# A hybrid decoder layer on one core: queries split two units ahead, sample steps emitted when their operands are due, and a planner that counts fp32 products as two passes

## The chip, the cores and the metric

The kernel runs on one core of a Trainium2 chip. The metric is the device time of one execution in microseconds; a time is the median of several runs. The engines are TensorE (PE, with its weight loads PEld), VectorE (DVE), ScalarE (ACT), GpSimd (POOL) and SyncE (SP, which here only issues DMAs). ACT and POOL issue DMAs too, in line with their other instructions.

## What is computed

One transformer-like layer for two groups of requests with the same weights: a prompt of 1024 tokens and 8 sample requests of 8 tokens, each with a cache of 4096 tokens in 32 pages. Cut to what matters:

```
h = rms_norm(x) * (1 + scale1) + shift1          # scale, shift, gate from the conditioning c
z = h @ w_in                                     # q, keys, values, gates, conv and pool inputs
k_cmp, v_cmp = compress(cache blocks of 32)      # silu(block @ w1) @ w2, for prompt and caches
o_cmp, p_cmp = attention over compressed blocks
top_i = the 16 best cache blocks of 64 by p_cmp  # samples; a prompt of 1024 has only 16 blocks
o_slc = attention over the selected blocks
o_win = attention over a window of 512
o_attn = g0 * o_cmp + g1 * o_slc + g2 * o_win
x = x + gate1 * (concat[o_attn, conv mixer, pooling mixer] @ w_out)
x = x + gate2 * swiglu(rms_norm(x) * (1 + scale2) + shift2)
```

All of it is float32. Products that need the precision are made as three products of rounded halves (`mm3`: high by high, high by low, low by high, on "float32r" tiles, whose names end in h, hi, l or lo); others are plain float32 products.

## The kernel before

The program has five stretches: the conditioning, the first norm and the input projection, with the compression of three caches (0 to 393 us of the profile); the attention (393 to 861); the output projection with the second norm; the product up of the FFN; the product down.

**Tasks and the planner's clock.** The program is written by generators ("tasks"). `run` always continues the task of the lowest priority number that is due by the planner's own clock: `self.t` holds a time for each engine, `use` adds the planner's cost of an operation to its engine, `mm` that of a product to "pe", and a task that yields a time is continued when that time is at most `MARGIN` (1.2 us) behind "pe". `hold` yields until a condition is true, `bank_of` until a PSUM bank is free. So the costs of the planner have no effect on the chip but through the order in which instructions are written. In the attention stretch that order is kept on PE (`self.turn`), and on DVE, ACT and POOL (the class `InTurn`), in the kernel before as well. Ahead of it and behind it the Tile scheduler orders the instructions.

**Prompt attention** (`prompt_attention`, `scores`): 32 units, for each of 8 blocks of 128 queries two halves of the heads, and for each half a unit "slc" (selected and compressed keys, tile `P`) and a unit "win" (window, tile `Pw`). A unit makes scores (`kh,qh`, `kl,qh`, `kh,ql`), masks them with DVE (`P<-bank`, with the running minimum in `st`), takes exponentials with ACT (`P<-P,st`), scales them with POOL (`P<-P,st` again), transposes with PE (`ident,P`), copies to `pt` with ACT or DVE, multiplies by values (`pt,vt`) and evacuates to `mo`, which goes to the DRAM tile `mix_d`. `query_parts` splits the queries of a block in `qh` (ACT) and `ql` (DVE).

**Compression** (`compress`, `compress_post`): eight pages at a time ("octet", tile `stream`, read by a gather of which SP's queue issues six pages and POOL's two) times `w1`; then an add (DVE), a silu (ACT, which loads a table for it), products by `w2`, a square root (another table), and key and value to `cmp_d`. Five of the eight caches are compressed during the attention.

**Sample attention** (`sample_select`, `sample_attention`, `sample_values`, `sample_combine`): for each of four pairs of requests, `sample_select` scores compressed keys, finds the blocks with a chain on DVE (`scr`, `mx8`, `bias`), then 9 units of cache or window are scored (`unit,qb`, `stream,qb`), exponentiated (`e`), transposed and multiplied by the values (`spt`), and `sample_combine` adds the 12 parts with weights (`cw`) into `co`, by one DVE instruction for each part, transposes it, and sends it (`smo`) to `mix_d`.

**Output projection** (`output_projection`): loads `wout` (tile `w_raw`, split into `w_hi` and `w_lo`), loads the mixer outputs back from `mix_d` (`mixc`, split into `mh` and `ml`), and x (`x1a`, `x1b`) by `x_load`.

Of the kernel before, what the change touches and what calls it, by code (L numbers as in the profile page):

```python
# [85 lines left out]
class Kernel:  # L86
# [43 lines left out]

    def ready(self, tag):

        return min(self.free[tag]) if self.free[tag] else self.t["pe"] + 0.25
# [16 lines left out]
    def mm(self, out, lhsT, rhs, start, stop, chain=False):  # L150
        n = 1
        for s in rhs.shape[1:]:
            n *= s
        if lhsT.dtype == F32:
            cost = 4 * max(n, 128) / 2400
            if lhsT.shape[-1] <= 64:
                cost *= 0.55 if lhsT.shape[-1] > 32 else 0.27
        else:
            cost = max(n, 256 if lhsT.dtype == F32R and n > 1 else n) / 2400
            if lhsT.shape[0] <= 64:  # L160
                cost *= 0.55
        self.t["pe"] += cost
        return self.in_turn(lhsT.shape[0] <= 64,
                            lambda: self.nc.tensor.matmul(out, lhsT, rhs, start=start, stop=stop, skip_group_check=chain))  # L164
# [393 lines left out]
    def gather(self, dst, name, b, p0, n, share=0):  # L558
# [10 lines left out]
        r = self.use("pool", share * 1.04, self.t["pe"])  # L569
# [8 lines left out]
    def compress(self, pool, batches, ahead):  # L578
# [5 lines left out]
        for b in batches:  # L584
# [5 lines left out]
            for half in range(2):  # L590
                uv = (yield from self.bank_of("S")).rearrange("p (v n) -> p v n", v=2)
                for q in range(2):
# [12 lines left out]
                    if i + 2 <= last:  # L605
                        self.compress_load(i + 2)
# [50 lines left out]
    def compress_post(self, pool, b, vt, pre, r, w=256):  # L657
        nc = self.nc
        nc.vector.tensor_tensor(pre[:, :, 0:w - 1], pre[:, :, 0:w - 1], vt[:, :, 1:w], op=OP.add)
        r = self.use("dve", 0.1 + w * 0.0023, r)  # L660
        nc.scalar.activation(vt[:, :, 0:w], pre[:, :, 0:w], AF.Silu, bias=self.pec[:, 0:1])
# [39 lines left out]
        self.give(self.cmp_tags[0], r)  # L701
        nc.vector.reciprocal(sq, sq)
# [348 lines left out]
    def prompt_attention(self, pool):  # L1051
        units = [(j, half, br) for j in range(8) for half in range(2) for br in ("slc", "win")]
        self.acc = None
        yield self.stacks_at
        for u, (j, half, br) in enumerate(units):
            if half == 0 and br == "slc":
                if j:
                    self.query_parts(self.query_pool, j)
            yield from self.scores(pool, u, j, half, br)

    def query_parts(self, pool, j):

        self.query_pool = pool
        self.qs = [pool.tile([P, 4, P], F32R, name=x, bufs=2) for x in ("qh", "ql")]
        self.split(*self.qs, self.q[:, :, j * P:(j + 1) * P], 512)
# [181 lines left out]
    def sample_select(self, pool, p, st):  # L1247
# [7 lines left out]
        yield from self.hold(lambda: self.cmp_done >= 2 * p + 2 and self.selected == p)  # L1255
# [17 lines left out]
        nc.scalar.activation(pc[:, 1:256], S[:, 0:NCMP], AF.Exp, bias=m0[:, 0:1], accum_out=m0[:, 1:2])  # L1273
        sn = pool.tile([P, 2, 64], F32, name="sn", bufs=2)
        for j, x in enumerate((8, 10)):
            nc.vector.tensor_tensor_reduce(out=sn[:, j], in0=S2[:, 64 * j:64 * j + 64], in1=self.m_new[:, p],
                                           scale=-1.0, scalar=3e38, op0=OP.add, op1=OP.min, accum_out=nm[:, x:x + 1])
        for j, x in enumerate((8, 10)):
            nc.scalar.activation(sn[:, j], sn[:, j], AF.Exp, scale=-1.0, bias=nm[:, x:x + 1], accum_out=den[:, x:x + 1])
        nc.vector.reciprocal(m0[:, 1:2], m0[:, 1:2])  # L1280
# [6 lines left out]
        r = self.use("dve", 2.0, self.t["pe"])  # L1287
        self.give("S", self.use("act", 1.0, self.t["pe"], table="exp"))
        self.give("S", r)
# [3 lines left out]
        self.mm(g[:, 32:96], self.rsum, i4, True, True)  # L1293
        ga = pool.tile([P, 3, 8], F32, name="ga", bufs=2)
# [32 lines left out]
        for b2 in range(2):  # L1327
            r = self.rows(b2)
            for h in range(2):
                n = P if h == 0 else NCMP - P  # L1330
                self.mm(o[r, 0:P], ct[:n, h, r], kv[b2][:n, h, P:2 * P], h == 0, h == 1)
        nc.scalar.activation(part[:, 11], o[:, 0:P], AF.Copy)
# [33 lines left out]
    def sample_attention(self, pool):  # L1366
# [9 lines left out]
        for u in range(36):  # L1376
            p, x = divmod(u, 9)
            st = sts[p]
            if x == 0 and p < 3:
                if p > 0:  # L1380
                    yield from self.hold(lambda: self.combined >= p)
# [54 lines left out]
    def sample_combine(self, pool, st, p):  # L1436
# [9 lines left out]
        for x, (a, b) in enumerate(br):  # L1446
            nc.vector.tensor_reduce(ds_[:, x:x + 1], nm[:, a:b], axis=AX.X, op=OP.min)
        for x, (a, b) in enumerate(br):
            nc.scalar.activation(w[:, a:b], nm[:, a:b], AF.Exp, scale=-1.0, bias=ds_[:, x:x + 1])
        nc.vector.tensor_tensor(dd[:, 0:11], w[:, 0:11], den[:, 0:11], op=OP.mult)  # L1450
# [7 lines left out]
        nc.vector.tensor_scalar(o, part[:, 11], gr[:, 0:1], None, op0=OP.mult)  # L1458
        for c in (0, 1, 2, 3, 4, 5, 6, 7, 8, 10):
            nc.vector.scalar_tensor_tensor(o, part[:, c], w[:, c:c + 1], o, op0=OP.mult, op1=OP.add)  # L1460
        yield self.use("dve", 3.7, self.t["pe"])
        yield from self.hold(lambda: "last" in st)
        nc.vector.scalar_tensor_tensor(o, part[:, 9], w[:, 9:10], o, op0=OP.mult, op1=OP.add)
        yield self.use("dve", 0.3, st["last_at"]) + 0.2
        tr = yield from self.bank_of("S")
        self.tr(tr[:, 0:P], o)
        mo = pool.tile([P, 4, 2, NT], F32, name="smo", bufs=2)
# [63 lines left out]
    def output_projection(self, wp, pool, nt, x1, opened):  # L1531
# [44 lines left out]
        def x_load(n=2):  # L1576
            for c, k in xq[:n]:
                dst, src = x1["load"](c, k)
                (nc.gpsimd if c == 0 else nc.scalar).dma_start(dst, src)
# [783 lines left out]
```

## Time and profile before

| | us |
|---|---|
| median of 3 runs (1707.48 to 1709.27) | 1708.68 |
| the profiled execution, its own time | 1700.77 |
| its span | 1699.2 |
| PE busy in the span | 1570.5 (92%) |
| DVE, ACT, POOL busy | 1098.5, 771.7, 665.4 |
| mean granted clock of TensorE | 0.962 |

PE is the engine that is busiest in each stretch. A PE that is not busy waits for another engine or a DMA. The granted clock is 1 at 2.4 GHz and 0.5 at 1.2 GHz. The profiled execution took 7.9 us less than the median of the timed runs.

### The profile page before, as it was taken

What the parts mean: (1) busy time and instruction counts of PE and PEld (TensorE: products, weight loads), DVE (VectorE), ACT (ScalarE), POOL (GpSimd) and SP (SyncE); (2) the same over time, 40 slices, a digit from 0 to 9 for tenths busy, and PEclk for the clock granted to TensorE, in tenths of its full rate; (3) what the DMA queues carried; (4) which work ended last, traced back from release to release, by engine and by line L of the source; (5) the groups of instructions that cost most, each with busy time, mean ns of one, the idle gap of its engine ahead of it and who ended that gap; (6) DMA issues with size and microseconds to landing.
All of it is one profiled execution on the core that took longest, in us unless ns stands there. A gap on an engine that the chain in (4) does not pass through costs nothing.

```text
span 1699.2 us, 35607 instructions
## 1 busy us (share of the span) xinstructions
PE 1570.5 (92%) x12697; PEld 1400.4 (82%) x12697; DVE 1098.5 (65%) x2638; ACT 771.7 (45%) x1821; POOL 665.4 (39%) x801
## 2 busy tenths in 40 slices
PE   6999999998897899899779989999999999899988
PEld 2988987897675666556479979999999999899988
DVE  4723354665564576766559887776777776476695
ACT  3521135324565566665548544333444343344462
POOL 3120111104332233322111365554555555688695
PEclk9899999998898999989989989999999999999999
DMA  9575756306464255234496735446444335967553
GB/s 342 195 260 165 199 173 214 128 10 193 141 187 137 79 160 174 78 103 130 156 328 213 235 131 191 147 143 230 144 144 144 143 141 202 390 240 242 189 172 120
DMA packets 183314, 302.12 MB, mean 178 GB/s; under 512 B 24305, under 2 KB 110898, under 8 KB 182818
## 3 DMA queue, kind: packets, MB, share of 16 engines
q1 hardware_dynamic: 163586, 270.96, 48.3%
q0 software_dynamic: 6624, 18.60, 3.5%
q10 hardware_dynamic: 12928, 10.29, 1.9%
q8 instruction: 101, 1.65, 0.4%
q14 instruction: 75, 0.61, 0.1%
HBM read 233.43 MB, written 70.53 MB: 179 GB/s over the span
## 4 chain that ended last, share of the span: by engine, by line
PE 69%; DVE 12%; DMA 6%; ACT 5%; issue 4%; POOL 2%; SPq 1%; ACTq 0%; DVEq 0%; POOLq 0%
PE bank L164 66%; PE bank L169 3%; DVE w_lo L208 2%; DMA stream<-in_cacheA 1%; DVE x L1918 1%; DVE P L78 1%; SPq L568 1%; DMA w_raw<-in_wup 1%; DMA x1b<-in_xT 1%; ACT Pw L78 1%; DMA wada<-in_wada 1%; ACT P L78 1%; POOL w_s L208 1%; DVE d_lo L208 1%; DVE pt L78 1%
## 5 line engine op out<-in xcount | busy, mean ns | idle before, releaser
L164 PE MATMUL bank<-b_lo,w_hi 128*128 128x272 f32 x1232 | 355.3, 290 | 2.5 <-DVE b_lo L208 2.5
L164 PE MATMUL bank<-b_hi,w_hi 128*128 128x272 f32 x1232 | 352.1, 291 | 5.3 <-DVE f_g L1716 2.9
L164 PE MATMUL bank<-b_hi,w_lo 128*128 128x272 f32 x1232 | 350.3, 290 | 1.2 <-DVE w_lo L208 1.2
L164 PEld LDWEIGHTS bank<-b_hi,w_hi 128*128 128x128 f32 x1232 | 231.8, 190 | 8.1 <-ACT b_hi L212 3.9
L164 PEld LDWEIGHTS bank<-b_lo,w_hi 128*128 128x128 f32 x1232 | 234.1, 190 | 3.4 <-DVE b_lo L208 3.4
L164 PEld LDWEIGHTS bank<-b_hi,w_lo 128*128 128x128 f32 x1232 | 232.3, 190 | 1.4 <-DVE w_lo L208 1.4
L208 DVE TENSOR_TENSOR w_lo<-w_raw,w_hi 128x512 fp32r<-128x512 f32 (+2 forms) x121 | 116.1, 970 | 64.0 <-ACT w_hi L212 63.5
L208 POOL TENSOR_TENSOR w_s<-w_raw 128x512 f32<-128x512 f32 (+1 forms) x88 | 125.0, 1421 | 69.9 <-DVE w_lo L208 52.7
L212 ACT ACTIVATE w_hi<-w_raw 128x512 fp32r<-128x512 f32 (+2 forms) x122 | 80.6, 678 | 148.3 <-PE bank L164 99.8
L164 PEld LDWEIGHTS bank<-stream 128*128 128x128 f32 x1056 | 131.9, 205 | 18.9 <-issue 10.5
L164 PE MATMUL bank<-stream 128*128 128x128 f32 x1056 | 137.6, 291 | 10.0 <-DMA stream<-in_cacheA 6.5
L208 POOL TENSOR_TENSOR x<-x,d_m 128x272 f32<-128x272 f32 x144 | 124.6, 885 | 36.5 <-DVE x L1918 20.2
L164 PE MATMUL bank<-h_hi,w_hi 128*128 128x384 f32 (+1 forms) x384 | 129.8, 338 | 0.0
L164 PE MATMUL bank<-g,w_hi 128*128 128x272 f32 x616 | 122.1, 294 | 6.6 <-DVE x L1918 5.4
L164 PE MATMUL bank<-h_hi,w_lo 128*128 128x384 f32 (+1 forms) x384 | 127.7, 333 | 0.0
L164 PE MATMUL bank<-h_lo,w_hi 128*128 128x384 f32 (+1 forms) x384 | 126.5, 329 | 0.0
L208 DVE TENSOR_TENSOR w_lo<-w_s,w_hi 128x512 fp32r<-128x512 f32 (+1 forms) x124 | 115.3, 933 | 15.6 <-ACT w_hi L212 13.4
L164 PE MATMUL bank<-g,d_hi 128*128 128x272 f32 x616 | 119.2, 290 | 4.5 <-DVE x L1918 2.3
L1918 DVE SCALAR_TENSOR_TENSOR x<-bank,mod,x 128x272 f32<-128x272 f32 (+1 forms) x192 | 86.6, 474 | 38.8 <-PE bank L164 35.6
L164 PEld LDWEIGHTS bank<-g,w_hi 128*128 128x128 f32 x616 | 98.7, 192 | 8.4 <-DVE x L1918 6.0
L1746 POOL TENSOR_TENSOR f_g<-f_g,f_v 128x272 f32<-128x272 f32 x44 | 44.0, 999 | 152.1 <-DVE f_v L1716 131.0
L78 POOL TENSOR_SCALAR P<-P,st 128x128 f32<-128x128 f32 (+14 forms) x120 | 63.7, 547 | 101.3 <-DVE st L78 91.8
(387 smaller groups left out, 3826.4 us busy)
## 6 DMA issues: line engine op xcount, KB each, us to landing
g_d<-f_s SPq DMA_DIRECT2D x57, 544.0 KB, 3.4
g<-g_d SPq DMA_DIRECT2D x56, 544.0 KB, 6.8
wada<-in_wada SPq DMA_DIRECT2D x96, 256.0 KB, 5.4
stream<-in_cacheA SPq DMA_DIRECT2D x192, 128.0 KB, 3.2
w_raw<-in_wup SPq DMA_DIRECT2D x40, 512.0 KB, 4.3
unit<-in_cacheB SPq DMA_DIRECT2D x152, 128.0 KB, 2.3
stream<-in_cacheB SPq DMA_DIRECT2D x104, 128.0 KB, 2.3
w_raw<-in_wout SPq DMA_DIRECT2D x24, 512.0 KB, 4.6
```

The source lines that it names most:

```text
L78: r = f(*args, **kwargs)
L164: lambda: self.nc.tensor.matmul(out, lhsT, rhs, start=start, stop=stop, skip_group_check=chain))
L169: return self.in_turn(ident.shape[0] <= 64, lambda: self.nc.tensor.transpose(out, in_, ident))
L208: (self.nc.vector if eng == "dve" else self.nc.gpsimd).tensor_tensor(out, a, b, op=op)
L212: self.nc.scalar.activation(hi, src, AF.Copy)
L568: eng.dma_start(dst[:, a + j, :], self.i[name][bass.ds(regs[j], 1)].rearrange("n p f -> (n p) f"))
L1746: nc.gpsimd.tensor_tensor(g[:, 1], s1, v, op=OP.mult)
L1918: nc.vector.scalar_tensor_tensor(out[:, :n], acc[:, :n], self.mod[:, 5, m, 0:1], out[:, :n], op0=OP.mult, op1=OP.add)
```

## The change

It has four parts, and none adds or removes an operation; two copies to `pt` go to DVE instead of ACT.

- The planner's costs: a plain float32 product is counted as two passes instead of four (`mm`), a page that POOL gathers as 0.6 us instead of 1.04 (`gather`).
- `when(t)`: a new yield until t less MARGIN, put ahead of steps of the compression and of the samples, so that they are written only when the planner's clock has come to their operands. The sums of `sample_combine` are written one at a time. The steps of `sample_select` are costed one by one, and their exponentials are written behind the masks.
- The queries of block j + 1 are split at the start of the second half of block j, two units ahead, instead of at the start of block j + 1.
- The wait until the pair before is combined moves from `sample_attention` (where it held up the units too) to the `sample_select` of the pair behind. All of `x_load` goes by POOL's queue; before it were the first four of 16, and ACT's queue took the other 12.

```
         if lhsT.dtype == F32:
-            cost = 4 * max(n, 128) / 2400
+            cost = 2 * max(n, 128) / 2400
...
+    def when(self, t):
+
+        yield t - MARGIN
...
-        r = self.use("pool", share * 1.04, self.t["pe"])
+        r = self.use("pool", share * 0.6, self.t["pe"])
...
                     if i + 2 <= last:
+                        yield from self.when(self.t["pe"])
                         self.compress_load(i + 2)
...
     def compress_post(self, pool, b, vt, pre, r, w=256):
         nc = self.nc
+        yield from self.when(r)
         nc.vector.tensor_tensor(pre[:, :, 0:w - 1], pre[:, :, 0:w - 1], vt[:, :, 1:w], op=OP.add)
         r = self.use("dve", 0.1 + w * 0.0023, r)
+        yield from self.when(r)
         nc.scalar.activation(vt[:, :, 0:w], pre[:, :, 0:w], AF.Silu, bias=self.pec[:, 0:1])
...
             if half == 0 and br == "slc":
-                if j:
-                    self.query_parts(self.query_pool, j)
+                self.qs = self.next_qs
+            if half == 1 and br == "slc" and j < 7:
+                self.query_parts(self.query_pool, j + 1)
...
-        self.qs = [pool.tile([P, 4, P], F32R, name=x, bufs=2) for x in ("qh", "ql")]
-        self.split(*self.qs, self.q[:, :, j * P:(j + 1) * P], 512)
+        self.next_qs = [pool.tile([P, 4, P], F32R, name=x, bufs=2) for x in ("qh", "ql")]
+        self.split(*self.next_qs, self.q[:, :, j * P:(j + 1) * P], 512)
...
-        yield from self.hold(lambda: self.cmp_done >= 2 * p + 2 and self.selected == p)
+        yield from self.hold(lambda: self.cmp_done >= 2 * p + 2 and self.selected == p and self.combined >= p - 1)
...
             if x == 0 and p < 3:
-                if p > 0:
-                    yield from self.hold(lambda: self.combined >= p)
                 self.spawn(1, self.sample_select(pool, p + 1, sts[p + 1]))
...
+        self.use("dve", 1.2, self.t["pe"])
         for c in (0, 1, 2, 3, 4, 5, 6, 7, 8, 10):
+            yield from self.when(self.t["dve"])
             nc.vector.scalar_tensor_tensor(o, part[:, c], w[:, c:c + 1], o, op0=OP.mult, op1=OP.add)
-        yield self.use("dve", 3.7, self.t["pe"])
+            self.use("dve", 0.28)
         yield from self.hold(lambda: "last" in st)
+        yield from self.when(st["last_at"])
...
-                (nc.gpsimd if c == 0 else nc.scalar).dma_start(dst, src)
+                nc.gpsimd.dma_start(dst, src)
```

Three places where the order of instructions moves. The first is ACT at the start of the second block of queries, in the attention's first microseconds. Before, the split `qh` stands behind the evacuations of an octet (`vt`), two table loads and the exponentials of the block ahead:

```order
L78 ACT_TABLE_LOAD
L78 ACTIVATE ksq<-bank,eps 128x256
L78 ACTIVATE vt<-bank 64x128 x4
L78 ACTIVATE mo<-bank 128x256
L78 DMA mix_d<-mo 128x2x128
L78 ACT_TABLE_LOAD
L78 ACTIVATE P,st<-P,st 128x128 x2
L78 ACTIVATE P,st<-P,st 128x7 x2
L78 ACTIVATE qh<-q 128x512
L78 ACTIVATE Pw,st<-Pw,st 128x128 x4
```

Now (the split of the same block, on ACT too):

```order
L78 ACTIVATE P,st<-P,st 128x128 x2
L78 ACTIVATE P,st<-P,st 128x7 x2
L78 ACTIVATE P,st<-P,st 128x128 x2
L78 ACTIVATE P,st<-P,st 128x7 x2
L78 ACTIVATE qh<-q 128x512
L78 ACTIVATE vt<-bank 64x128 x4
L78 ACTIVATE Pw,st<-Pw,st 128x128 x4
L78 ACTIVATE P,st<-P,st 128x128 x2
L78 ACTIVATE P,st<-P,st 128x7 x2
L78 ACTIVATE pt<-bank 7x512
L78 ACT_TABLE_LOAD
```

`qh` has gone ahead of the table loads and of the exponentials of the second half of its predecessor.

The second place is DVE in the first `sample_combine`, in the middle of the attention (`cw` the weights, `co` the sum, `Pw,st<-bank` the mask of a prompt unit's scores, `ISA st` the read of its minimum). Before:

```order
L78 TENSOR_TENSOR cs<-cs,gr 128x2
L78 TENSOR_SCALAR cw<-cw,cs 128x9
L78 TENSOR_SCALAR cw<-cw,cs 128x2
L78 TENSOR_SCALAR co<-part,gr 128x128
L78 SCALAR_TENSOR_TENSOR co<-part,cw,co 128x128 x10
L78 ISA Pw,st<-bank,m_edge 128x320
```

Now (on DVE, the last part of the same combine):

```order
L78 SCALAR_TENSOR_TENSOR co<-part,cw,co 128x128
L78 ISA e,nm<-bank,bias 128x512
L78 ISA nm 128x1
L78 RECIPROCAL ksq<-ksq 128x256
L78 SCALAR_TENSOR_TENSOR kvo<-ko,c_kgain,ksq 128x2x128
L78 SCALAR_TENSOR_TENSOR co<-part,cw,co 128x128
L78 COPY pt<-bank 128x8x64 x2
L78 RECIPROCAL st<-st 128x2
L78 TENSOR_TENSOR st<-st,gates 128x2
L78 RECIPROCAL st<-st 128x2
L78 TENSOR_TENSOR st<-st,gates 128x2
L78 SCALAR_TENSOR_TENSOR co<-part,cw,co 128x128 x8
```

The ten sums stood in one run; now sample masks, a key's normalisation, copies to `pt` and steps of `st` stand between the first of them, and the last eight are a run still.

The third place is POOL at the end of the attention (`P` and `Pw` are the scalings of the last two prompt units, `smo` the samples' result, `x1a` and `x1b` the loads of x, `mixc` the loads of the mixer outputs that the first projection products need). Before:

```order
L78 TENSOR_SCALAR P<-P,st 128x1024 x2
L78 DMA mix_d<-smo 128x4x16
L78 TENSOR_SCALAR P<-P,st 128x1024 x2
L78 TENSOR_SCALAR Pw<-Pw,st 128x640 x2
L78 TENSOR_SCALAR Pw<-Pw,st 128x63 x2
L78 TENSOR_SCALAR Pw<-Pw,st 128x640 x2
L78 TENSOR_SCALAR Pw<-Pw,st 128x63 x2
L78 DMA mix_d<-smo 128x4x16
L1553 DMA mixc<-mix_d 128x2x272 x4
L1579 DMA x1a_10598<-in_xT 128x2x272 x4
```

Now (POOL, the same place):

```order
L78 TENSOR_SCALAR P<-P,st 128x1024 x2
L78 DMA mix_d<-smo 128x4x16
L78 TENSOR_SCALAR P<-P,st 128x1024 x2
L1600 DMA x1a_10598<-in_xT 128x2x272 x4
L1600 DMA x1a_10599<-in_xT 128x2x272 x4
L1600 DMA x1b<-in_xT 128x2x272 x6
L78 TENSOR_SCALAR Pw<-Pw,st 128x640 x2
L78 TENSOR_SCALAR Pw<-Pw,st 128x63 x2
L78 TENSOR_SCALAR Pw<-Pw,st 128x640 x2
L78 TENSOR_SCALAR Pw<-Pw,st 128x63 x2
L1574 DMA mixc<-mix_d 128x2x272 x4
L1600 DMA x1b<-in_xT 128x2x272 x2
```

Fourteen loads of x stand ahead of the last four scalings, the samples' result has left ahead of the last `P`, and no `smo` stands behind the scalings any more.

## Rows read from the trace of the kernel before

**Rows 1.** Busy time of each engine in six stretches of the span (columns: stretch and its length; for each engine busy us and instructions; granted clock; busy share of the DMA engines; GB/s).

```profile
0.00:100.00 100.00, 83.38 (x536) 63.28 (x537) 52.01 (x101) 41.69 (x81) 24.58 (x38) 0.95 0.77 266
100.00:393.00 293.00, 278.44 (x1889) 253.73 (x1887) 134.57 (x206) 86.14 (x158) 39.46 (x68) 0.98 0.52 158
393.00:841.00 448.00, 395.99 (x3954) 279.29 (x3954) 280.68 (x1192) 266.38 (x740) 134.74 (x244) 0.93 0.46 138
841.00:1020.00 179.00, 151.44 (x1119) 148.50 (x1120) 148.19 (x309) 97.31 (x224) 59.50 (x63) 0.90 0.69 228
1020.00:1450.00 430.00, 428.12 (x3403) 426.12 (x3402) 312.75 (x486) 168.83 (x340) 219.57 (x195) 1.00 0.47 166
1450.00:1699.20 249.20, 233.11 (x1803) 229.44 (x1802) 170.26 (x345) 111.31 (x281) 187.56 (x196) 0.98 0.65 222
```

**Rows 2.** What PE waited for between 393 and 841 us (waiting engine, what it was to write, its line, what it waited for: us in total, times, longest us).

```profile
PE bank L164 <- ACT qh L78: 21.0, 7, 5.3
PE bank L164 <- DVE pt L78: 6.3, 5, 2.7
PE bank L169 <- ACT pt L78: 3.5, 2, 2.8
PE bank L164 <- ACT vt L78: 3.2, 1, 3.2
...
PE bank L164 <- DVE ql L78: 1.8, 2, 1.5
```

**Rows 3.** The timeline of all engines around the first of the seven waits for `qh`, and PE's next wait of over 1 us (columns: start us, length us, engine, line, operation; in brackets the engine's idle time ahead of it and what ended it).

```profile
419.20 3.84 PE L164 MATMUL bank<-stream 128*128 128x128 f32 x32
...
426.06 1.28 ACT L78 ACT_TABLE_LOAD   x1 [0.48 <-ACT mo L78]
...
427.36 0.40 ACT L78 ACTIVATE P<-P,st 128x128 f32<-128x128 f32 x1
...
428.71 0.61 ACT L78 ACTIVATE qh<-q 128x512 fp32r<-128x512 f32 x1
...
429.36 0.69 DVE L78 TENSOR_TENSOR ql<-q,qh 128x512 fp32r<-128x512 f32 x1 [3.01 <-ACT qh L78]
429.38 0.63 PE L164 MATMUL bank<-kh,qh 64*128 64x320 f32 x2 [5.27 <-ACT qh L78]
...
447.16 0.65 PE L164 MATMUL bank<-pt,vt__286 128*64 128x256 f32 x4 [2.67 <-DVE pt L78]
```

**Rows 4.** The five stretches at half clock that follow a wait for `qh`, and the sum over all eleven stretches at half clock behind a wait in the attention (columns as in rows 1; the sum names its engines).

```profile
428.00:434.80 6.80, 5.42 (x26) 4.21 (x27) 4.15 (x24) 5.34 (x28) 0.00 (x0) 0.50 0.26 82
...
537.20:544.00 6.80, 5.24 (x26) 2.98 (x28) 4.46 (x18) 0.10 (x2) 1.73 (x3) 0.50 0.10 39
588.40:595.20 6.80, 5.40 (x38) 3.76 (x39) 2.96 (x15) 3.98 (x11) 0.00 (x0) 0.50 0.07 5
...
690.80:694.20 3.40, 3.40 (x25) 2.51 (x22) 2.83 (x15) 0.53 (x2) 0.85 (x2) 0.51 0.00 0
...
752.30:755.70 3.40, 3.30 (x12) 1.70 (x14) 2.51 (x8) 0.61 (x2) 0.54 (x2) 0.50 0.48 190
sum 61.20, PE 53.34 PEld 36.08 DVE 40.02 ACT 33.04 POOL 12.20; mean PE 4.85 PEld 3.28 DVE 3.64 ACT 3.00 POOL 1.11
```

**Rows 5.** The timeline around the first `sample_combine` (columns as in rows 3).

```profile
607.05 0.81 ACT L78 ACTIVATE P<-P,st 128x640 f32<-128x640 f32 x1
...
608.63 3.45 DVE L78 SCALAR_TENSOR_TENSOR co<-part,cw,co 128x128 f32<-128x128 f32 x9
...
609.30 1.05 ACT L78 ACTIVATE pt<-bank 128x512 f32<-128x512 f32 x2
...
609.92 1.59 PE L169 MATMUL bank<-ident,Pw 64*128 64x64 f32 x16 [2.81 <-ACT pt L78]
```

**Rows 6.** The timeline of POOL at the end of the attention (columns as in rows 3).

```profile
808.03 2.21 POOL L78 TENSOR_SCALAR P<-P,st 128x1024 f32<-128x1024 f32 x2 [0.34 <-DVE st L78]
811.42 2.19 POOL L78 TENSOR_SCALAR Pw<-Pw,st 128x640 f32<-128x640 f32 x4 [1.18 <-DVE st L78]
...
853.06 0.80 POOL L78 DMA_DIRECT2D mix_d<-smo  x1 [36.48 <-DVE smo L78]
853.85 2.84 POOL L1553 DMA_DIRECT2D mixc<-mix_d  x4
856.69 2.11 POOL L1579 DMA_DIRECT2D x1a<-in_xT  x3
```

**Rows 7.** The timeline of the other engines at the end of the attention (columns as in rows 3; ACTq is ACT's queue of DMAs).

```profile
801.25 0.68 DVE L78 CUSTOM_DVE_ANT_0 P<-bank,m_slc 128x512 f32<-128x512 f32 x1
...
850.12 1.15 ACT L212 ACTIVATE w_hi<-w_raw 128x512 fp32r<-128x512 f32 x2 [2.35 <-DMA w_raw<-in_wout]
...
851.39 0.34 DVE L78 SCALAR_TENSOR_TENSOR co<-part,cw,co 128x128 f32<-128x128 f32 x1
...
851.79 0.48 PE L169 MATMUL bank<-ident,co 128*128 128x128 f32 x1 [11.37 <-DVE co L78]
...
852.88 2.44 ACTq L1579 DMA_DIRECT2D x1a<-in_xT  x4
...
860.61 1.50 PE L164 MATMUL bank<-mh,w_hi 128*128 128x272 f32 x5 [8.34 <-ACT mh L212]
```

**Rows 8.** PE's products with `stream` between 100 and 393 us, the compression in the projection's stretch (columns: operation, shapes, count; busy us, mean ns; idle before and its releasers).

```profile
L164 PE MATMUL bank<-stream 128*128 128x128 f32 x448 | 56.8, 284 | 8.6 <-DMA stream<-in_cacheA 5.2 <-ACT stream L198 2.9 <-DVE cy L848 0.6
```

More of the change, by code (lines that the diff above doesn't have):

```diff
@@ L701, in compress_post @@
         self.give(self.cmp_tags[0], r)
+        yield from self.when(r)
         nc.vector.reciprocal(sq, sq)
@@ L1272, in sample_select @@
         nc.vector.memset(pc[:, 256:257], 0.0)
-        nc.scalar.activation(pc[:, 1:256], S[:, 0:NCMP], AF.Exp, bias=m0[:, 0:1], accum_out=m0[:, 1:2])
+        t = self.use("dve", 0.35, self.t["pe"] + 0.1)
         sn = pool.tile([P, 2, 64], F32, name="sn", bufs=2)
@@ L1277, in sample_select @@
                                            scale=-1.0, scalar=3e38, op0=OP.add, op1=OP.min, accum_out=nm[:, x:x + 1])
+        t2 = self.use("dve", 0.3)
+        yield from self.when(t)
+        nc.scalar.activation(pc[:, 1:256], S[:, 0:NCMP], AF.Exp, bias=m0[:, 0:1], accum_out=m0[:, 1:2])
+        self.use("act", 0.5, t + 0.1, table="exp")
         for j, x in enumerate((8, 10)):
             nc.scalar.activation(sn[:, j], sn[:, j], AF.Exp, scale=-1.0, bias=nm[:, x:x + 1], accum_out=den[:, x:x + 1])
+        t = self.use("act", 0.66, t2 + 0.1)
+        yield from self.when(t)
         nc.vector.reciprocal(m0[:, 1:2], m0[:, 1:2])
@@ L1286, in sample_select @@
         nc.vector.tensor_reduce(i4, im.rearrange("p (j c) -> p j c", c=4), axis=AX.X, op=OP.add)
-        r = self.use("dve", 2.0, self.t["pe"])
-        self.give("S", self.use("act", 1.0, self.t["pe"], table="exp"))
-        self.give("S", r)
+        r = self.use("dve", 1.3, t + 0.1)
+        self.give("S", t)
+        self.give("S", t)
         yield r + 0.8
@@ L1293, in sample_select @@
         self.mm(g[:, 32:96], self.rsum, i4, True, True)
+        yield from self.when(self.t["pe"])
         ga = pool.tile([P, 3, 8], F32, name="ga", bufs=2)
@@ L1331, in sample_select @@
                 self.mm(o[r, 0:P], ct[:n, h, r], kv[b2][:n, h, P:2 * P], h == 0, h == 1)
+        yield from self.when(self.t["pe"])
         nc.scalar.activation(part[:, 11], o[:, 0:P], AF.Copy)
@@ L1447, in sample_combine @@
             nc.vector.tensor_reduce(ds_[:, x:x + 1], nm[:, a:b], axis=AX.X, op=OP.min)
+        yield from self.when(self.use("dve", 0.3))
         for x, (a, b) in enumerate(br):
             nc.scalar.activation(w[:, a:b], nm[:, a:b], AF.Exp, scale=-1.0, bias=ds_[:, x:x + 1])
+        yield from self.when(self.use("act", 0.5, table="exp") + 0.1)
         nc.vector.tensor_tensor(dd[:, 0:11], w[:, 0:11], den[:, 0:11], op=OP.mult)
@@ L1466, in sample_combine @@
         self.tr(tr[:, 0:P], o)
+        yield from self.when(self.t["pe"])
         mo = pool.tile([P, 4, 2, NT], F32, name="smo", bufs=2)
```

## The prediction

> **What bounds the kernel now.** I read the stretches first [rows 1]: PE is busy 1570.5 us of 1699.2, and where it isn't is uneven. In the FFN's product up it idles 1.9 us of 430 and runs at full clock: nothing can be won there by order. In the attention it idles 448.0 - 396.0 = 52.0 us, at a granted clock of 0.93, while DVE, ACT and POOL are busy for 281, 266 and 135 of the 448 us. None of these is full, so PE's idle time there is a matter of who stands behind whom. Between 841 and 1020 it idles 27.6, at 0.90. Then I read what PE waited for in the attention [rows 2]: one row is 40% of it, the seven waits for `qh`, 21.0 us, and 1.8 more for `ql`. The rest, 52.0 - 22.8 - 0.6 (the 0.6 us of the end that lies before 841) = 28.6 us, has many causes; `pt` and `vt` are 6.3 + 3.5 + 3.2 = 13.0 of it.
>
> The timeline shows why `qh` is late [rows 3]. The split needs only queries that exist since the projection. But it is written at the start of its block, and ACT runs what was written ahead of it first: a table load of 1.28 us, four exponentials for `P`, then `qh` at 428.71. PE starts 0.06 us behind its end, after 5.27 us of nothing.
>
> A wait costs twice: behind five of the seven waits the granted clock is 0.5 for 3.4 to 6.8 us [rows 4]. PE was busy 5.42 + 5.24 + 5.40 + 3.40 + 3.30 = 22.8 us in these. If that work took half at the full clock, the loss is 11.4 us. All eleven such stretches hold 53.3 us of PE's work, so the other six hold 30.5 and lose 15.3.
>
> The sample steps show the second pattern [rows 5]. `sample_combine` puts one run of ten sums on DVE, 3.45 us for nine; PE's transposes need `pt`, whose copies ACT can start only at 609.30, behind the exponentials for `P` of a later unit, while DVE is shut. PE waits 2.81 us.
>
> The third place is the end [rows 7]: PE waits 11.37 us for `co`, because the sums stand between splits of `w_out`, which wait for landings (2.35 us in the row of `w_hi`), and then 8.34 us for `mixc`, which POOL's queue can fetch only once `smo` has left [rows 6]. That is 19.7 us.
>
> **The change, part by part.** *Queries, two units ahead.* The same 0.61 us on ACT and 0.69 on DVE, eight times, earlier. The second pair of buffers is free then, as the last block's scores are done by the second half. So the seven waits go: at most 22.8 + 11.4 = 34.2 us. At least nothing: ACT still has the table loads and exponentials ahead of what PE needs next. How much of the gain stays depends on the next wait, and those are rare: 52 us of idle time in 448. Behind the first wait PE ran for 15 us before another of over 1 us, from 429.4 to 447.16 - 2.67 = 444.5 [rows 3]. What it does there (more scores, sample scores, an octet of 3.84 us of products, rows 3) asks nothing of ACT's late queue, and during these ACT catches up. I take 70% of 34.2: **-24**.
>
> *`when` and the halved cost of fp32 products.* The planner's clock was about right: 16 products of an octet are 32 instructions and take 3.84 us [rows 3], 0.24 each, where the formula said 0.21. Now it says 0.11. So where the new clock leaves room of 1 us between a step and what needs it, PE holds up to 2 us of real work, as long as there is other work to put there. No instruction gets faster. The pool of gain is the other waits, 28.6, and their clock, 15.3: 43.9 together. Bounds: -44, and 0 or above if the room for samples is taken from the prompt's steps. In the new order the copies to `pt`, the largest of these waits, have no more room than before, and the last eight sums of `co` are one run still. I take 30%: **-13**.
>
> *The end.* The samples finish ahead of the last prompt units, so the 11.37 us for `co` can't come last any more. In their place stand fourteen loads of x on POOL ahead of the last four scalings of `Pw`. In the trace a load takes POOL 2.11 / 3 = 0.70 us [rows 6], so 9.8 in all; `Pw`'s scalings, which began at 811.42, 1.2 us behind the last of `P`, would be 8.6 later, and behind them stand transposes, `pt`, values, `mix_d`, then `mixc` (8.34 as before). Also PE had other work from there to 840.4 (851.79 - 11.37), the samples' among it, that hid those steps. The samples' part is now done earlier, so the same steps stand barer. Bounds: -11.4 (the loads leave while POOL would have waited for ACT's exponentials) to +8.6 (the loads are felt whole, and the bare steps take what `co` took). I take **-1.5**, the sum of -11.4, of the 8.6 and of 1.3 for the bare steps, the least certain term.
>
> The Trainium skill, PSUM — Partial Sum Buffer (section "Engine vs sequencer instructions"), says that the queues of ScalarE, VectorE and GpSimdE are strict FIFO. The trace agrees: `mixc` left POOL only behind a `smo` that had waited for 36.48 us. By this rule alone, without the -11.4, the end would be 8.6 us slower and the whole sum 10.1 us smaller, which the range holds.
>
> *Twelve loads of x from ACT's queue to POOL's.* 2.44 / 4 = 0.61 us each on ACT, 0.70 on POOL [rows 6, 7]: 8.4 us more on POOL, which between 841 and 1020 is busy 59.5 of 179 us [rows 1], so they are hidden beyond the fourteen costed above. If that cover were gone, it would be 12 x 0.09 = 1.1 us. The skill's DMA: Bandwidth & Descriptors ("Issuing engine by pattern") gives simple loads to Sync, and 1 us against 0.6 to a first byte; an estimate by that page is 0.4 us once. No row here shows it.
>
> *The front and the FFN.* The front holds 8.6 us of waits at `stream` [rows 8], mostly for gathers, and the order of the octets changes there. Bounds: -8 (nearly all of them) to +6 (two octets side by side wait 3 us each). I take **-2**. The FFN's order stays within a few swaps of neighbours; 0, with 2 us to both sides, from idle times of 1.9 and 16.1 [rows 1].
>
> **Sum.** -24 - 13 - 1.5 - 2 = -40.5. The profiled execution took 1700.8; so the changed one 1660.3. The median lies 7.9 above its profile, and 1708.7 - 40.5 = **1668**. Own range: queries from -15 to -34, samples from -3 to -25, the end -11 to +9, as independent terms, some 18 around it: 1650 to 1686.
>
> **Rivals.**
> *The gains are given back.* ACT stays as late as it was; PE runs its scores 5 us earlier and then waits at `ident,P` for exponentials that still come at the old time. For it: `qh` stood behind just these exponentials. Against it: few waits follow. With a third of the queries' gain (-11), 10% of the others (-4) and the end at +3 it is -12: 1697.
>
> *Slower: the samples' work is spent too early.* Their products are what PE does while a prompt unit's softmax is under way; from the first mask of a unit (801.25) to its scaled `P` (808.03 + 2.21 = 810.24) there are 9.0 us [rows 6, 7]. Counting fp32 as half makes the planner put more of this work behind each wait, so it runs out sooner. Each unit left without it bares up to 9.0 us. It decides from 40.5 / 9.0 = 4.5 units on; with six it is +13.5: 1722. Against it: in the new order the sample products reach to the last two units of 32. For it: those two are bare now, at the place where POOL's queue is longest.
>
> *Nothing changes.* The chip's waits follow ACT's and DVE's real lateness, which no cost of the planner knows, and shift by a few us: 1708. Against it: the seven waits have one cause, which is gone.
>
> **How the numbers follow.** Gain as summed, or more, 0.68; given back, 0.13; nothing, 0.06; slower, 0.13. What a measurement of this kernel can tell from no change is about 0.2%, 3.4 us. Faster 0.68 + 0.13 = 0.81; same 0.06; slower 0.13. The range reaches from 1645, below which I leave 0.08 (most of the 78 us of waits and clock in the attention gone), to 1706, above which lie no more than the two last cases with 0.12 of their 0.19, some of "nothing" ending within it.
>
> **What would show it.** Right: no wait of PE for `qh` or `ql` in the attention (22.8 before); a granted clock there of 0.95 or more (0.93); the attention's PE idle at 25 to 35 us (52); no `ident,co` wait at the end, and `mh,w_hi` still waited for, by 15 to 25 us in the last steps together, with fourteen loads ahead of `Pw` on POOL. The FFN alike within 2 us. Wrong: new waits of PE for `P` exponentials or `pt` that sum up to as much as `qh` did; a bare stretch of PE over 30 us at the attention's end; octets in the front that wait for gathers by more than 8.6 us.

## The result, and the profile after

The changed kernel takes 1699.5 us (median of 10 runs, 1695.7 to 1706.8); the kernel before took 1709.0 beside it (10 runs, 1704.7 to 1713.6). The ratio is 0.9946, with a 95% interval of 0.9929 to 0.9963: 9.5 us faster, where 40.5 were forecast. The direction is right, but three quarters of the gain are missing, and the time lies inside the outer range alone (1645 to 1706), not inside the prediction's own (1650 to 1686).

The stretches of the changed kernel from 100 us on (columns as in [rows 1]):

```profile
100.00:393.00 293.00, 272.46 (x1822) 246.82 (x1822) 130.99 (x191) 84.73 (x152) 36.77 (x58) 0.97 0.50 152
393.00:841.00 448.00, 395.24 (x3948) 281.03 (x3946) 290.62 (x1225) 262.89 (x730) 148.47 (x265) 0.93 0.51 151
841.00:1020.00 179.00, 163.05 (x1212) 156.30 (x1213) 147.50 (x298) 101.79 (x231) 61.64 (x63) 0.91 0.64 207
1020.00:1450.00 430.00, 426.86 (x3390) 424.46 (x3389) 311.81 (x483) 168.85 (x340) 220.46 (x197) 1.00 0.47 165
1450.00:1697.20 247.20, 231.37 (x1791) 228.19 (x1789) 171.62 (x345) 111.05 (x279) 187.52 (x194) 0.98 0.65 221
```

Between 393 and 841 PE idles 52.8 us at 0.93, against 52.0 at 0.93 [rows 1]. Nothing seems to have changed there. What it waits for has (columns as in [rows 2], 393 to 860 us):

```profile
PE bank L168 <- DVE pt L78: 9.7, 7, 3.0
PE bank L173 <- POOL Pw L78: 6.8, 1, 6.8
PE bank L173 <- ACT e L78: 5.6, 2, 5.3
PE bank L168 <- ACT w_hi L216: 5.6, 1, 5.6
PE bank L173 <- DVE st L78: 5.4, 6, 2.0
PE bank L173 <- POOL P L78: 4.2, 5, 1.7
PE bank L168 <- ACT pt L78: 4.0, 4, 2.0
```

No row for `qh` or `ql` is left of 22.8 us. In their place stand waits for `e`, `st`, `P` and `pt` that were not there or were shorter (rows of before for `P`, `e` and `st` stand under before_again). The front tells another part: the first score starts at 398.2 us, not at 391.2 as before, with as many octets compressed ahead of it. Two of PE's waits in it (timeline, columns as in [rows 3]):

```profile
287.81 1.65 PE L168 MATMUL bank<-h_sq,mean_h 128*128 128x384 f32 x2 [4.20 <-ACT h_sq L804]
...
319.29 1.06 PE L168 MATMUL bank<-wada,sc 128*32 128x256 f32 x2 [6.35 <-DMA wada<-in_wada]
```

And the end, from the timeline of the changed kernel (POOL, ACT and PE):

```profile
826.34 5.79 POOL L1600 DMA_DIRECT2D x1a<-in_xT  x8
...
837.40 4.35 POOL L78 TENSOR_SCALAR Pw<-Pw,st 128x640 f32<-128x640 f32 x8
841.19 1.97 PE L173 MATMUL bank<-ident,Pw 64*128 64x64 f32 x32 [6.83 <-POOL Pw L78]
...
856.22 0.43 ACT L216 ACTIVATE mh<-mixc 128x272 fp32r<-128x272 f32 x1 [2.43 <-DMA mixc<-mix_d]
...
858.25 3.21 ACT L216 ACTIVATE w_hi<-w_raw 128x512 fp32r<-128x512 f32 x6
...
858.92 0.59 PE L168 MATMUL bank<-mh,w_hi 128*128 128x272 f32 x1 [5.57 <-ACT w_hi L216]
```

This is the end as forecast. The fourteen loads of x hold POOL from 826.3 to 837.4, PE waits 6.83 us for the scalings behind them, and then 5.57 us for a `w_hi` that stands on ACT behind an `mh` whose `mixc` has not landed. The wait of 11.37 us for `co` [rows 7] is gone.

One trace is not enough to place 9.5 us. The profiled execution of before took 7.9 us less than the median, so the kernel before was profiled once more (before_again, below). All comparisons of stretches that follow are with that second trace unless they name rows.

### The profile page after: what moved, and what is told of

Its sections match the earlier page's. It is cut to its first block, busy times and chain, and to the rows that moved or that the text cites. A ratio compares the mean times of both kernels' runs of the same rounds, so it can differ in the third digit from the quotient of the medians.

```text
span 1697.2 us, 35639 instructions
## 1 busy us (share of the span) xinstructions
PE 1572.0 (93%) x12697; PEld 1400.0 (82%) x12697; DVE 1104.8 (65%) x2645; ACT 771.4 (45%) x1814; POOL 679.1 (40%) x813
## 4 chain that ended last, share of the span: by engine, by line
PE 66%; DVE 13%; DMA 7%; ACT 4%; issue 4%; POOL 3%; SPq 1%; ACTq 0%; POOLq 0%; DVEq 0%
PE bank L168 63%; PE bank L173 3%; DMA wada<-in_wada 2%; DVE P L78 2%; DVE w_lo L212 1%; DVE x L1939 1%; POOL w_s L212 1%; DMA w_raw<-in_wup 1%; DVE Pw L78 1%; SPq L572 1%; DMA mixc<-mix_d 1%; DVE st L78 1%; ACT P L78 1%; DMA x<-x_d 1%; DVE b_lo L212 1%
```

## The experiments

First the two traces of the same program.

**before_again**: the kernel before, unchanged.

> The kernel before, unchanged, for a second trace of it. The first one had 346.5 us from the first h_hi product to the first score, where two kernels with the same front had 349.3 and 351.3, and the changed kernel 353.5. If the first trace was a low one by chance: 349 to 352 us here, so that the changed front costs some 3 us and not 7. If not: 345 to 348.

Measured: 1709.5 us, profiled at 1712.4. The attention with its end, from the first score to the first projection product (396.3 to 871.0), in columns as in [rows 1]:

```profile
396.30:871.00 474.70, 404.44 (x3970) 283.13 (x3969) 291.15 (x1220) 273.45 (x754) 143.47 (x256) 0.90 0.47 143
```

PE's waits for `qh` and `ql` in it, and those for `P`, `e` and `st` at its transposes:

```profile
PE bank L164 <- ACT qh L78: 19.8, 7, 5.2
...
PE bank L169 <- POOL P L78: 3.5, 3, 2.0
...
PE bank L164 <- DVE ql L78: 2.1, 2, 1.8
...
PE bank L169 <- ACT e L78: 1.5, 2, 1.1
...
PE bank L169 <- DVE st L78: 0.2, 1, 0.2
```

The same stretch in the first trace (391.2 to 860.6):

```profile
391.20:860.60 469.40, 397.48 (x3969) 280.33 (x3968) 291.34 (x1220) 272.98 (x754) 142.56 (x256) 0.91 0.48 144
```

The waits are alike, but the same products were 7 us longer, at a lower granted clock (0.90 for 0.91). So the stretch of one trace is good to some 5 us, whatever its waits say. The front, from the first product with `h_hi` to the first score, took 349.9 us here, so the changed kernel's 353.5 is some 4 us longer and not 7.

**The parts alone.** Three parts of the change put on the kernel before, each by itself, and the first of them taken back in the changed kernel.

q_only, on the kernel before:

```
             if half == 0 and br == "slc":
-                if j:
-                    self.query_parts(self.query_pool, j)
+                self.qs = self.next_qs
+            if half == 1 and br == "slc" and j < 7:
+                self.query_parts(self.query_pool, j + 1)
```

> The kernel before, with the queries split two units ahead and nothing else of the change. Theory A (the waits for qh are a delay of their own, and most of the 34 us of wait and clock is kept; new waits come from the other parts): the attention with its end 20 to 28 us shorter than the 469.4 us of before, the time 20 to 28 us under before. Theory B (the split only showed how late ACT is; the same lateness comes back at pt, P and e within the next steps): no wait for qh, other waits in the attention up from 28.7 to 40 us or more, the time 3 to 12 us under before. The front stays at 346.5 us from the first h_hi product to the first score, in both.

cost_only, on the kernel before: `cost = 2 * max(n, 128) / 2400` in `mm`.

> The kernel before, with fp32 products counted as two passes and nothing else. Theory A (the new clock breaks as much as it mends, and is what made the other waits longer): the attention with its end 5 us longer or more, waits other than qh at 35 us or more. Theory B (more real work between producer and consumer): waits other than qh under 25 us, the time 5 to 15 us under before. If the front's 7 us are the clock's, the front is 350 to 357 us here.

when_only, on the kernel before: every `when`, the steps of `sample_select` costed one by one, the sums of `co` one at a time, the moved hold. (The cost of a gather and the queue of the loads of x were not tried alone.)

> The kernel before, with the steps of compression and samples written only when due, the sums of co one at a time and the moved hold, and nothing else (fp32 products still four passes, split at the start of the block, gather and x loads as before). Theory A (this is the useful part for the sample steps): waits other than qh under 24 us of 28.7, the time 5 to 12 us under before. Theory B (it moves steps about, no net gain): within 4 us of before. If the front's 7 us are its, the front is 350 to 357 us here.

after_q_late, the changed kernel with the diff of q_only reversed.

> The changed kernel with the split back at the start of the block. Theory A (in this order too the early split is worth most of the waits it removes): 15 to 28 us slower than the changed kernel, so 6 to 18 us slower than before. Theory B (the clock at half and the steps one by one leave ACT so much room that qh is hardly waited for): within 5 us of the changed kernel, waits for qh under 8 us.

| kernel | us | ratio to before (95%) | profiled execution, us | attention and end in it, us | PE busy in it | PE idle |
|---|---|---|---|---|---|---|
| before_again | 1709.5 | 1.0002 (0.9982 to 1.0021) | 1712.4 | 474.7 | 404.4 | 70.3 |
| q_only | 1707.7 | 0.9995 (0.9978 to 1.0012) | 1713.4 | 477.8 | 405.0 | 72.8 |
| cost_only | 1701.9 | 0.9966 (0.9945 to 0.9986) | 1713.0 | 478.7 | 407.5 | 71.2 |
| when_only | 1717.8 | 1.0045 (1.0024 to 1.0067) | 1718.8 | 486.3 | 405.7 | 80.7 |
| changed kernel | 1699.5 | 0.9946 (0.9929 to 0.9963) | 1698.9 | 460.7 | 399.3 | 61.4 |
| after_q_late | 1686.6 | 0.9870 (0.9845 to 0.9894) | 1685.7 | 451.4 | 391.6 | 59.8 |

The early split alone brings next to nothing, 1.3 us: its waits are those of theory B, its time is less than even theory B allowed. Taken out of the changed kernel it brings 13 us: outside both theories of after_q_late. cost_only is 7.1 us faster, in the range of its theory B; its row of the table comes from an execution 11.1 us above its median, so it says little of where the gain lies. when_only is 8.8 us slower, outside both of its theories. PE's waits in the attention and end of q_only:

```profile
PE bank L169 <- DVE st L78: 14.9, 7, 6.0
...
PE bank L169 <- POOL P L78: 8.0, 5, 3.3
PE bank L169 <- ACT e L78: 6.5, 5, 3.2
```

`qh` and `ql` are gone from its rows, and the waits for `st`, `P` and `e` at the transposes are 29.4 us, where before_again has 5.2. At this point the prediction's argument that few waits follow one for `qh` seemed to have fallen: as if PE, no longer held up by `qh`, waited as long for the next late thing.

**The split alone, in an unchanged order.** But q_only changes more than the split. `query_parts` also charges the planner's clock, 0.5 us of "act" and 0.6 of "dve", and the planner draws a new order from there: by the traces, nearly half of PE's instructions in the attention of q_only stand elsewhere than before. So the next two kernels write the split early and keep the charge where it was; in their attention every other instruction stands where it stood, which the traces bear out for PE, DVE, ACT and POOL.

before_q_moved, on the kernel before (after_q_moved: the same on after_q_late):

```
             if half == 0 and br == "slc":
                 if j:
-                    self.query_parts(self.query_pool, j)
+                    self.use("dve", 0.06 + 512 * 0.00107, self.use("act", 0.09 + 512 * 0.00084))
+                self.qs = self.next_qs
+            if half == 1 and br == "slc" and j < 7:
+                kept = dict(self.t)
+                self.query_parts(self.query_pool, j + 1)
+                self.t = kept
```

> The kernel before with qh and ql written two units earlier on ACT and DVE, while the planner's clock is charged for them where it was, so that in the attention every other instruction stands exactly as before. Theory A (q_only gained nothing because the planner reshuffled the rest): 15 to 24 us under before. Theory B (PE gets ahead of ACT and DVE by what it no longer waits, and waits the same time for st, P, e and pt): no wait for qh, other waits up by 15 us or more, within 6 us of before.

> The kernel after_q_late (1686.6 us, 12.9 us of waits for qh and ql) with qh and ql written two units earlier in the same way, all else in its attention in the same order. Theory A (the early split itself is good, and the 13 us that the changed kernel lies over after_q_late are the reshuffle that its cost on the planner's clock brings): 5 to 15 us under after_q_late, 1672 to 1682. Theory B (an early split itself costs in this order, since ACT and DVE do it while PE waits for them): 1692 to 1702, as the changed kernel. In between, within 4 us of after_q_late: the waits only change their place.

before_q_moved took 1677.9 us, ratio 0.9809 (0.9789 to 0.9829): 31.6 us faster than before, more than the 24 that the prediction gave the split. after_q_moved took 1673.7, ratio 0.9788 (0.9768 to 0.9809): 12.9 us under after_q_late. Theory A in both, though before_q_moved gained more than its 15 to 24. The stretch of before_q_moved:

```profile
395.30:840.00 444.70, 387.58 (x3970) 272.65 (x3969) 290.38 (x1220) 272.58 (x754) 142.72 (x256) 0.94 0.50 152
```

Against before_again it is 30.0 us shorter. PE's idle time is 57.1 us instead of 70.3, so 13.2 of the 21.9 us of `qh` and `ql` stay away and 8.7 are waited elsewhere. And PE is busy 387.6 us instead of 404.4 with the same products, at a granted clock of 0.94 instead of 0.90. By these two traces the clock gives back more (16.9) than the waits. Both were taken of executions some 3 us above the median of their kernel. Against the first trace of before, 7.9 under its median, PE idles 14.8 us less and is busy 9.9 less: that both shrink is sure, which of them by more is not. Its largest waits are those of the end and of `pt`, as before:

```profile
PE bank L169 <- DVE co L78: 11.4, 1, 11.4
PE bank L164 <- ACT mh L212: 8.4, 1, 8.4
PE bank L164 <- DVE pt L78: 6.8, 5, 2.7
PE bank L169 <- ACT pt L78: 3.5, 2, 2.8
```

PE's largest waits in the attention of after_q_late:

```profile
PE bank L168 <- ACT pt L78: 14.4, 5, 12.0
PE bank L168 <- ACT qh L78: 11.5, 6, 4.3
PE bank L168 <- DVE pt L78: 9.9, 7, 4.0
PE bank L173 <- POOL Pw L78: 9.2, 1, 9.2
```

and of after_q_moved:

```profile
PE bank L168 <- ACT pt L78: 14.0, 4, 12.0
PE bank L168 <- DVE pt L78: 9.8, 7, 3.9
PE bank L173 <- POOL Pw L78: 9.1, 1, 9.1
```

The large rows are the same, without `qh`; some smaller ones have come, of 2 us or less each. The stretch of after_q_moved:

```profile
397.50:836.30 438.80, 386.72 (x3970) 275.82 (x3969) 296.53 (x1240) 270.73 (x750) 153.51 (x268) 0.95 0.54 163
```

PE's idle time falls from 59.8 us to 52.1, so 7.7 of the 12.9 us of `qh` and `ql` stay away. The comparison also prices the rest of the change. With the split out of the way it is worth 1677.9 - 1673.7 = 4 us; with the split late it is worth 1709.0 - 1686.6 = 22 us. One reason is that the rest had already cut the waits for `qh` (11.5 us for 19.8; the halved cost alone, in cost_only, has 9.7): the two parts cure the same wait, so their gains don't add. But both differences are between two orders, and the next experiments show how little that says.

**Where the charge stands, or which order comes out.** Between the changed kernel and after_q_moved lie 26 us, and the only difference in their sources is where the split's cost is charged. Two kernels charge it nowhere (after_q_free: the `use` line of the diff left out) and at both places (after_q_both: `kept` left out).

> The changed kernel (split written two units ahead) with the split's cost charged to the planner's clock nowhere. The changed kernel charges it where it writes it (1699.5 us), after_q_moved where the block starts (1673.7). Theory A (a charge at the block's start is what helps, because it makes the planner leave room for the block's first scores and masks): without it 1693 to 1705, like the changed kernel. Theory B (a charge in the block's middle is what hurts): 1670 to 1680. Theory C (each order that comes out is one of many, and their times scatter by 10 us or more whatever the reason of the nudge): anything, 1680 to 1692 as well.

> The changed kernel with the split's cost charged at both places. Theory A (the charge at the block's start helps): 1668 to 1680. Theory B (the one in the middle hurts): 1693 to 1705. Theory C (scatter of orders): anything between.

after_q_free: 1686.0 us (ratio 0.9866, 0.9847 to 0.9886), which only theory C allows. after_q_both: 1678.1 (0.9816, 0.9800 to 0.9833), in the range of theory A. So by its place the charge helps at the block's start (1686.0 to 1673.7, 1699.5 to 1678.1) and hurts in its middle (1686.0 to 1699.5, 1673.7 to 1678.1). That looks like a cause. To see whether it is one, the margin of the planner was nudged with the charge at either place: `MARGIN = 1.3`, `1.0` and `1.5` on the changed kernel, `1.0` and `1.5` on after_q_moved. (`run` continues a task once "pe" is at least MARGIN past the time that the task yielded, not at most, as the description of the planner has it. So a larger margin leaves a little more room behind steps that yield their end; it does so with the charge at either place.)

> The changed kernel with MARGIN at 1.3 us instead of 1.2: a nudge that moves a few hundred instructions by a few places for no reason of its own. It measures how far an order of this planner is from its neighbour. If a single order is within 3 us of its neighbours, differences of 10 us between orders have causes worth naming one by one; if it is 6 us or more off the changed kernel's 1699.5, a part of each difference here is which order came out.

> The changed kernel (charge in the block's middle, 1699.5 us) with MARGIN at 1.0 instead of 1.2, which reorders about as many instructions as moving the charge does. Theory A or B (the charge's place is what costs 26 us): 1692 to 1707. Theory C (orders scatter): it may come out anywhere from 1670 to 1710.

> The changed kernel with MARGIN at 1.5. As for after_m10: by the charge's place 1692 to 1707, by scatter anywhere from 1670 to 1710.

> The kernel after_q_moved (charge at the block's start, 1673.7 us) with MARGIN at 1.0. By the charge's place 1668 to 1682; by scatter anywhere from 1665 to 1705.

> The kernel after_q_moved with MARGIN at 1.5. By the charge's place 1668 to 1682; by scatter anywhere from 1665 to 1705.

| MARGIN | charge in the middle, us (ratio) | charge at the start, us (ratio) |
|---|---|---|
| 1.2 | 1699.5 (0.9946) | 1673.7 (0.9788) |
| 1.3 | 1700.3 (0.9948, 0.9930 to 0.9965) | |
| 1.0 | 1694.0 (0.9927, 0.9902 to 0.9952) | 1692.5 (0.9912, 0.9880 to 0.9944) |
| 1.5 | 1690.5 (0.9904, 0.9872 to 0.9935) | 1687.2 (0.9898, 0.9866 to 0.9929) |

The nudge to 1.3 moved, by the traces, under a third as many instructions as the charge does, and the time by 0.8 us; by its expectation that would have spoken for causes worth naming. The larger nudges overrule it. Those to 1.0 and 1.5 reorder some three quarters as many as the charge or more, and at either of them the two groups lie within 3.3 us, not 26, with executions that overlap. One of the nudged kernels with the charge at its good place is 18.8 us slower than after_q_moved. So most of the 26 us is theory C: orders that this planner draws for the same work, with the same parts in them, scatter between 1674 and 1700 us, and the changed kernel's order is one of the slowest of them. In all three pairs the charge at the start is the faster, by 25.8, 1.5 and 3.3 us, so an effect of the place of a few us is not excluded by seven kernels.

**The end.** late_end, on after_q_late (`self.ends` holds the last instruction of the attention on DVE, ACT and POOL):

```
-                    r = self.split(hi, lo, t[:, k], HALF, at)
+                    with self.tc.issue_after(self.ends[0]), self.tc.issue_after(self.ends[1]):
+                        r = self.split(hi, lo, t[:, k], HALF, at)
...
-                nc.gpsimd.dma_start(dst, src)
+                with self.tc.issue_after(self.ends[2]):
+                    nc.gpsimd.dma_start(dst, src)
```

> The kernel after_q_late with the loads of x on POOL put behind the last scaling of Pw, and the splits mh and ml behind ACT's and DVE's last instruction of the attention. Its end holds two waits of PE, 9.2 us for Pw (behind twelve loads of x) and 12.0 us for pt (behind mh that waits for mixc). Theory A (both are a matter of position): both gone, the end's idle 25.8 us down to 8 or less, 1686.6 - 14 to - 20, so 1667 to 1673. Theory B (what follows is late anyway: mh, w_hi and the last mixc come as late as before): 1681 to 1687.

It took 1684.2 us (0.9853, 0.9833 to 0.9873), 2.4 under after_q_late. The attention with its end is 18.8 us shorter (432.6 us for 451.4): both waits went, as theory A says, but the time is that of theory B. The output projection behind it is 118.0 us up to the first product of the FFN, where it was 101.0: `w_hi` now stands behind the splits `mh` that wait for `mixc`, PE waits 11.8 us for it where it waited 1.6, and the same products are 7.5 us longer, at a granted clock of 0.92 for 0.98.

```profile
PE bank L168 <- ACT w_hi L216: 11.8, 3, 5.8
```

The gain was given back one stretch later.

moved_x, on after_q_moved, has the second half of this diff alone.

> The kernel after_q_moved (1673.7 us) with the loads of x put on POOL behind the last scaling of Pw, and no other thing; mh and ml stay where they were. Its end has 9.1 us of waits for Pw behind the loads and 12.0 for pt behind mh. If the loads are a cost of their own: the wait for Pw at 1 us or less, 1673.7 - 6 to - 9. If what stands behind them (pt behind mh, which waits for mixc) takes their place: the wait for pt at 18 us or more and 1671 to 1676.

It took 1668.0 us, ratio 0.9757 (0.9737 to 0.9777): 5.7 us under after_q_moved, and the fastest kernel of this study, 41 us under before and 31 under the changed kernel. Its waits:

```profile
PE bank L168 <- DVE pt L78: 12.4, 8, 3.9
PE bank L168 <- ACT pt L78: 10.4, 4, 8.4
...
PE bank L173 <- POOL Pw L78: 2.5, 1, 2.5
```

and POOL's end in it:

```profile
804.29 3.32 POOL L78 TENSOR_SCALAR Pw<-Pw,st 128x640 f32<-128x640 f32 x4 [2.03 <-ACT mh L216]
807.56 5.81 POOL L1605 DMA_DIRECT2D x1a<-in_xT  x8
```

The wait for `Pw` fell from 9.1 us to 2.5, and that for `pt` did not take its place (ACT's longest 8.4 for 12.0, DVE's in all 12.4 for 9.8). So the twelve loads of x that stood on POOL ahead of the scalings cost about 6 us in this order; in the changed kernel's own it was not tried.

## Why the prediction was wrong

The step that failed is the sum's first: that the change's diff to `query_parts` is a move of 14 instructions, to be priced by the wait it removes. In place of its -24 stands +12.9: so much slower is the changed kernel than after_q_late, which lacks this part alone. The other parts together, after_q_late against before, are -22.4, where the sum had -16.5; and 12.9 - 22.4 is the measured -9.5. The mechanism of the price was right: before_q_moved, where the part is no more than that move, gained 31.6 us, between the 24 taken and the bound of 34.2. But in this kernel the same line also charges a planner, and the whole attention is drawn anew. The prediction compared the orders, saw `qh` ahead, and took the waits of the old order as those of the new one. q_only shows that they are not: 29 us of waits for `st`, `P` and `e`, where the old order had 5. Two of the prediction's own signs had said so in the trace of the changed kernel: a granted clock of 0.93 where 0.95 was asked for, and PE idle for 52.8 us where it was to be 25 to 35. My rival "the gains are given back" named the outcome (-12; measured -9.5), but not the cause. It said that ACT stays late and PE waits at the transposes instead. Such waits came, but with the order kept, in before_q_moved, only 8.7 of 21.9 us are waited elsewhere. So that the time lies within the outer range is luck: the prediction left room there for other mechanisms, not for this one.

*The clock's part of the split*, 11.4 us at most, was of the right size or too small: PE is busy 16.9 us less in before_q_moved by the second trace of before, 9.9 by the first. In q_only nothing of it came (405.0 us for 404.4).

*The sample steps*, -13: not confirmed. In the changed kernel the waits in the attention other than `qh`, `ql` and the end are 61.4 - 17.3 = 44.1 us (the end's 17.3 are PE's waits from 826 to 858.9), where before_again has 70.3 - 21.9 - 20.0 = 28.4. I had taken 30% off them; they grew by half. But not by these steps alone: after_q_late has them too, in another order, and there the same waits are 59.8 - 12.9 - 22.8 = 24.1 us (the 22.8 are its last three large waits, 9.2 for `Pw`, 12.0 for `pt` and 1.6 for `w_hi`). Alone, the new yields cost 8.8 us (when_only against 1709.0), the halved cost brought 7.1 (cost_only), and both with the rest 4 once `qh` is out of the way; each of these is a single draw, and less than the scatter of draws. That the planner leaves more room does not mean that the room lies where a wait was.

*The end*, -1.5: right, in size and in mechanism. 19.7 us before, 17.3 now, so -2.4; `co` gone, the loads of x in its place, as the rule of the strict FIFO queues had it (the Trainium skill, PSUM — Partial Sum Buffer, section "Engine vs sequencer instructions"); the trace agrees with 11.0 us of loads ahead of the scalings, of which PE waited 6.8.

*The front*, -2: wrong side, within its bounds. +3.6 us against before_again, with waits behind ACT's copies of `stream` and for a late `wada`; not tested further. Four traces with the order of the front before (the two of before, q_only, before_q_moved) have 346.5 to 351.3 us, and eight with the changed one 350.0 to 355.8, so some 3 us are left of it.

*The FFN*, 0: right. From its first product up to the end 737.7 us after and 738.6 in before_again.

*The rival that was slower*, the samples' work spent too early: seen in its beginnings only. The last of its products with values ends at 812 us instead of 840, and the last units run bare, but the end costs no more than before.

What stays open: why a given order is good. Between orders with the same parts lie up to 26 us, and I can name each wait in one of them, but not a rule by which the planner would have avoided it. So the 9.5 us are what this draw of the changed kernel gained; how far orders of the kernel before scatter was not measured.

## What to carry to other kernels

Where a planner or scheduler writes the order, an edit that "moves" a step is two edits: the move, and a new draw of the whole order. Price the first from the trace; for the second measure a few neutral nudges, and believe no difference smaller than their scatter. To get the move alone, keep the planner's clock as it was and write only the instruction elsewhere: here that was worth three times the change. Two remedies for the same wait don't add: find out what each leaves of it.

## What the runs showed of the hardware

Scattered waits cost more than themselves. In before_q_moved 21.9 us of waits went, 8.7 came back elsewhere, and the same products ran 16.9 us shorter, with the granted clock at 0.94 for 0.90. That second cost differs from run to run: two traces of the same program, with like waits, had PE busy for 397.5 and 404.4 us in the attention, and against the shorter one the 16.9 is 9.9.

A plain DMA of 272 columns issued by POOL holds its queue for 5.79 / 8 = 0.72 us, and the instructions behind it wait: in the changed kernel fourteen loads stood ahead of POOL's last scalings for 11.0 us, and PE waited 6.83 us for these scalings.
